# A decoder layer on one core: w_ada requests from ACT's queue to SP's, two norms two units later, and another order of window keys, exponentials and sums in the sample attention

## The chip, the cores and the metric

The kernel runs on one core of one Trainium2 chip. The core has five engines, each with a queue of its own: TensorE (PE, which multiplies matrices), VectorE (DVE), ScalarE (ACT), GpSimd (POOL) and SyncE (SP, used here only to request transfers). Transfers are carried by 16 DMA engines that all queues share. An engine that requests a transfer does so as an instruction in its own queue, and what is behind that instruction waits until it has gone out. The metric is the device time of one execution in microseconds, as the median over several runs.

## The reference

One step of a one-layer decoder. A prompt group (512 tokens) and a sample group (8 sequences of 8 new tokens, each with 2048 cached tokens in pages) go through the same weights: adaLN modulation and RMS norm, one wide input projection, two attention branches in parallel (forgetting attention, "FoX", and native sparse attention, "NSA", with a compressed, a selected and a sliding part), a gated mix, an output projection and a squared-ReLU MLP. Cut to what bears on this change:

```python
mod = einsum('bd,de->be', silu(c), w_ada) + b_ada          # shift, scale, gate of both norms
h   = rms_norm(x, norm1_g) * (1.0 + sc1) + sh1
z   = einsum('btd,dc->btc', h, w_in)

# each sample sequence: cached pages and the window's state
fox_all = concatenate([gather_pages(fox_pool, page_table), fox_rows])
nsa_all = concatenate([gather_pages(nsa_pool, page_table), nsa_rows])
kc, vc  = compressed_kv(nsa_all[:, :, 0], nsa_all[:, :, 1])      # compression of blocks of 32 tokens
o_fox   = softmax(fox_q . fox_k + cumulative log forget) . fox_v
o_nsa   = gate0 * o_compressed + gate1 * o_selected + gate2 * o_window   # window: last 512 tokens

mix = g_fox * (o_fox @ w_br_fox) + g_nsa * (o_nsa @ w_br_nsa)
x   = x + gt1 * (mix @ w_out)
y   = x + gt2 * (relu(norm2(x) @ w_up) ** 2 @ w_down)
```

At 8 sequences with 2048 cached tokens the selected part and the forgetting part read all keys of a sequence, 4 MB together.

## The kernel before

The program runs through stages, mostly one after the other on PE: a first stage that compresses the cached rows of the 8 sequences (to about 155 us), the input projection (to 285), the prompt attention (to 405), the sample attention (to 562), and then mix, output projection and MLP (to the end). Within each engine a scheduler puts instructions in order ahead of time; the code fixes an order between two instructions where it matters with `issue_after`, and the order written out in tables sets the rest. At run time every queue is strictly in order. A transfer on a hardware queue (SP and ACT) takes the next of eight semaphores in turn, and its request waits until the transfer that used the semaphore before has landed.

**First stage.** Its work is 48 units `u`, each twelve matmuls `hid` on half of the key or value rows of one or two sequences. ACT rounds the cached rows (`xh<-cpg`), DVE makes the remainder (`xl<-cpg,xh`). Other work is hung on the units by the table `todo` (from line 584 on): the adaLN matrix is multiplied in eight chunks of 1 MB (`ada_first`, in the order 4, 0, 5, 1, 6, 2, 7, 3, at units 27, 29, 32 and so on), each with a load of weights `wada` two chunks ahead (`ada_first_load`, two buffers), a copy `adap` on ACT and a turn `adat` on PE one unit later. In the same table stand the RMS norms of the five x tiles: `norm(k)` squares and sums a tile on ACT (`sq`), takes the root on DVE and scales on ACT (`x<-x,nrs`); `turned(k)` turns the tile on PE (`nt`) and copies it on ACT (`adw<-nt`). The rows of the last sequence's pages (`cpg`, eight loads of 128 KB) are requested by SP after the last x tiles.

**Sample attention.** `sample_attention` (line 1597) runs a loop over the sequences `b` = 0 to 7. The cached rows lie in three rooms (`fr` and `sr`, 2 MB each), so the loads of `b + 3` follow the last use of `b`. For each `b`: PE makes the scores `ss` (`sequence_scores`, line 1770, on 32 x 32 pieces), then scores with the new tokens `sn`; DVE takes the maximum and negates it; ACT takes the exponentials `sS`; PE turns the weights (`spn`, `sp`), ACT copies them (`spT`), and PE multiplies with the values (`so`). Meanwhile DVE turns the keys of the next sequence in place (`fr<-fr`, `sr<-sr`, one instruction for each quarter and each branch, and `oT<-D3b` for the log forget counts, copied to `CT` by ACT). All of these turns must be done before the next scores start.

The sliding window is done for two sequences at a time, at even `b`: PE turns the keys (`wk<-wr`, `window_keys`), ACT copies them (`wkt`), PE scores (`sw`, `window_scores`), DVE takes the maximum (line 1877), ACT takes the exponential (`scr<-scr,swst`, `window_weights`). `sequence_end` and `window_end` scale what `so` left for the sequence of two turns ago and for the window of the pair before (`OA`, `OAw`); the next values overwrite that bank, so `so` waits for them.

Of the kernel before, what the change touches and what calls it, by code (L numbers as in the profile page):

```python
# [10 lines left out]
AF = mybir.ActivationFunctionType  # L11
OP = mybir.AluOpType
# [33 lines left out]
class Step:  # L46
# [55 lines left out]
    def ts(self, out, a, s1, s2, op0, op1=None, **kw):  # L102
        if op1 is None:
            self.last_ts = self.nc.vector.tensor_scalar(out, a, s1, s2, op0=op0, **kw).ins
        else:
            self.nc.vector.tensor_scalar(out, a, s1, s2, op0=op0, op1=op1, **kw)

    def stt(self, out, a, s, b, op0, op1):
        return self.nc.vector.scalar_tensor_tensor(out, a, s, b, op0=op0, op1=op1)
# [135 lines left out]
    def late_constants(self):  # L245
        nc, I, ts, c, jp, field = self.nc, self.I, self.ts, self.const_tile, self.jp, self.field
        field("t_row", [(OP.bitwise_and, 7)])
        nc.vector.memset(c("ones", [P, P]), 1.0)
        field("prow", [])
        field("p_hi", [(OP.arith_shift_right, 3)])  # L250
        field("p31", [(OP.bitwise_and, 31)])
        field("g_row", [(OP.bitwise_and, 63), (OP.arith_shift_right, 5)])
        h_row = field("h_row", [(OP.bitwise_and, 63), (OP.arith_shift_right, 3)])

        sl = c("slope_i", [P, 1], I32)
        ts(sl, h_row, -1.0, 126.0, OP.mult, OP.add)
        ts(sl, sl, 23, None, OP.logical_shift_left)
        self.slope = sl.bitcast(F32)
        ts(c("identB", [P, P], BF16), jp, 0.0, None, OP.is_equal)
        ts(c("diagB", [P, P], BF16), jp, 0.0, NEG, OP.is_gt, OP.mult)  # L260
        ts(c("triU", [P, P]), jp, 0.0, None, OP.is_ge)
# [53 lines left out]

    def ada_first_load(self, pe, ch):
        w = self.adas[ch] = pe.tile([P, NK, 256], F32, tag="big", bufs=2, name=f"wada{ch}")
        if ch in (4, 0):
            self.ada_load(ch, w)
            return  # L320
        with self.tc.issue_after(self.last_high):
            self.ada_load(ch, w, "scalar")

    def ada_first(self, pe, ch):
        part = pe.tile([P, 256], F32, tag="adap", bufs=2, name=f"adap{ch}")
# [196 lines left out]
    def first_stage(self, pl, pe, hf):  # L522
# [12 lines left out]
        def norm(k):  # L535
            with self.tc.issue_after(self.last_high):
                self.norm_scaled(xs[k], 0, k, xs[k], pl.tile([P, D], BF16, tag="csx", name=f"sq{k}"))
            self.flipped = self.rooted

        def turned(k):  # L540
            t0, m = TILES[k]
            for h in range(2):
                self.act(hf[:, 4 * h:4 * h + 4, t0:t0 + m], self.norm_turned(xs[k], 0, k, h))
# [40 lines left out]
        todo = {u: [] for u in range(48)}  # L584
# [2 lines left out]
        todo[16] += [pinned(self.cmp_second_half)]  # L587
        todo[10] += [self.constants_turned, self.ada_turned, lambda: ends.update(b=self.cmp_bias(pe))]
        todo[12] += [lambda: self.cmp_bias_end(ends["b"])]
        for k, (n, u) in enumerate(((21, 24), (23, 26), (25, 28), (30, 32), (31, 33))):  # L590
            todo[n] += [lambda k=k: norm(k)]
            todo[u] += [lambda k=k: turned(k)]

# [18 lines left out]
        for k, u in enumerate((27, 29, 32, 34, 36, 38, 40, 42)):  # L612
            todo[u] += [lambda k=k: ends.update({k: self.ada_first(pe, ada[k])})]
            todo[u + 1] += [lambda k=k: ends[k]()]
            if k < 6:
                todo[u] += [wada(k + 2)]
            if k % 2:
                todo[max(u + 2, 34)] += [lambda k=k: self.modulate(0, hf, range(k - 1, k + 1)),
                                         lambda k=k: self.dma("gpsimd", self.hfd[:, k - 1:k + 1], hf[:, k - 1:k + 1])]
        self.lfg = {}  # L620
        for y, u in enumerate((34, 37)):
# [975 lines left out]
    def sample_attention(self, sp, ctx):  # L1597
# [37 lines left out]
        for b in range(NB):  # L1635
            n, odd = b // 2, b % 2
            if b and b + 2 < NB:
                self.key_prep(b + 2)
            self.sequence_scores(b, (lambda: self.values(b - 1, range(2, 4))) if b == last else None)
            if not odd and b:  # L1640
                for o in range(2):
                    self.window_keys(b + o)
            self.new_scores(b)
            if not odd:
                self.window_new(n)
            if not odd and b:
                self.values(b - 1, range(1, 4))
            if b == last:
                self.hL = self.keep.tile([P, 5 * D], F32R, tag="r2", bufs=1, name="hL2")[:, 0:NK * NT].rearrange("p (k t) -> p k t", k=NK)
                self.hH = self.rp.tile([P, NK, NT], F32R, tag="rp", name="hH")  # L1650
                self.tokens_load(range(4), self.CT[0:1, 0:4, None])
            self.sequence_max(b)
            if odd:
                self.window_turned(n)
            if b > 1:
                self.sequence_end(b - 2)
                if not odd:
                    self.window_end(n - 1)
            if b < last:
                with self.tc.issue_after(self.last_stat):  # L1660
                    self.key_turn(b + 1, (0, 1))
            if 0 < b < last and odd:
                self.values(b - 1, range(2, 4))
            if b == last - 1:
                self.mix_ahead()
            if odd:
                self.window_values(n)
                if b < last:
                    for o in range(2):
                        self.window_load(b + 1 + o, "gpsimd")  # L1670
                if b > 1:
                    self.pair_sums(n - 1)
            if b and b + 2 < NB:
                self.sample_load(b + 2, range(1 if b % 2 == 0 else 2, 4))
            if b < last:
                with self.tc.issue_after(self.last_stat):
                    self.key_counts(b + 1)
                    self.key_turn(b + 1, (2, 3))
            if b == last:
                self.sequence_end(b - 1)  # L1680
                self.window_end(n)
                ctx.close()
                self.mix_open()
                with self.tc.issue_after(self.last_exp):
                    self.w0 = self.gate_weights(0, 0)
            if b == 0:
                for o in range(2):
                    self.window_keys(o)
            if not odd and b:
                self.window_scores(n)  # L1690
            self.turn_weights(b)
            if b < last:
                with self.tc.issue_after(self.last_weights):
                    self.act(self.CT, self.ct)
            if b < last:
                self.values(b, range(1 if odd else 2))
            if b + 3 < NB:
                self.sample_load(b + 3, range(1 if odd else 2))
            if not odd:
                if b == 0:  # L1700
                    self.window_scores(n)
                self.window_weights(n)
            if b == 0:
                with self.tc.issue_after(self.last_stat):
                    self.sample_maps(maps)
# [146 lines left out]
    def sequence_end(self, b):  # L1852

        mx, dn, nm = self.stat.pop(b)
        d = self.small.tile([P, 1], F32, tag="sd", name=f"sd{b}")
        self.nc.vector.tensor_reduce(d, dn, axis=AX.X, op=OP.add)
        self.nc.vector.reciprocal(d, d)
        col = 128 * (b % 2)
        self.ts(self.OA[b % 2], self.sob[:, col:col + 64], d, self.GA[:, b:b + 1], OP.mult, OP.mult)

    def sums(self, b, sel, OA, first):

        for g in range(2):
            self.mm(self.acc[64 * g:64 * g + 64, 64 * b:64 * b + 64], OA, sel[g], first, not first)
# [14 lines left out]
    def window_weights(self, i):  # L1879
        st = self.wst[i]  # L1880
        self.tt(st[:, 2:3], st[:, 0:1], st[:, 1:2], OP.max)
        self.last_stat = self.nc.vector.tensor_scalar(st[:, 2:3], st[:, 2:3], -1.0, None, op0=OP.mult).ins
        self.act(self.SWt, self.SWt, AF.Exp, bias=st[:, 2:3], accum_out=st[:, 3:4])

    def window_turned(self, i):
        tb, tn = self.trb(f"spw{i}"), self.mmb(f"spwn{i}")
# [14 lines left out]
    def window_end(self, i):  # L1901
        st, col = self.wst.pop(i), 256 + 128 * (i % 2)
        self.nc.vector.reciprocal(st[:, 3:4], st[:, 3:4])
        w = self.OAw[i % 2]
        self.ts(w, self.sob[:, col:col + 64], st[:, 3:4], self.GB[:, 1, i:i + 1], OP.mult, OP.mult)
        self.stt(w, self.sob[:, col + 64:col + 128], self.GB[:, 0, i:i + 1], w, OP.mult, OP.add)

    def mix_open(self):

# [638 lines left out]
```

## Time and profile before

| | us |
| --- | --- |
| median of three runs | 1173.26 (1171.53 to 1177.72) |
| profiled execution | 1177.12 |
| its span | 1175.5 |
| first stage, 0 to 155: PE busy | 122.4 of 155 |
| input projection, 155 to 285: PE busy | 128.3 of 130 |
| prompt attention, 285 to 405: PE busy | 115.0 of 120 |
| sample attention, 405 to 562: PE busy | 142.3 of 157, mean granted clock 0.86 |
| rest, 562 to 1175.5: PE busy | 607.6 of 613.5 |

The profile is taken on one execution. A row of its timeline is: start, duration, engine, line, operation, output <- inputs, shape, how many instructions are merged into the row, and in brackets how long the engine had stood idle before it and what ended the idle time. "PEclk" and "granted clock" are the share of full speed at which TensorE was clocked. A busy PE at half clock is busy, but does half the work.

### The profile page before, as it was taken

Reading aid. Unit: us, or ns where it says so; the run is one execution under the profiler, and the core shown is the slowest. Engines: PE = TensorE matmul, PEld = TensorE weight load, DVE = VectorE, ACT = ScalarE, POOL = GpSimd, SP = SyncE. Lnnn points to the kernel's source line nnn. Section 1 sums busy time; section 2 is a strip of 40 time slices with the busy share of each in tenths; the row PEclk is TensorE's granted clock in tenths of the full one; section 3 lists DMA queues with packets and bytes.
Section 4 is the critical chain, followed back from the end, with each engine's and each line's share of the span. In section 5 each row is a group of like instructions: output and inputs, shape, how many; then the busy total and the mean of one; then the engine's idle time right before and its main releaser. Section 6 shows DMA issues by size and latency. Waiting matters only on the chain.

```text
span 1175.5 us, 24506 instructions
## 1 busy us (share of the span) xinstructions
PE 1115.5 (95%) x9161; PEld 950.5 (81%) x9161; DVE 779.3 (66%) x1904; ACT 524.9 (45%) x1107; POOL 241.5 (21%) x332
## 2 busy tenths in 40 slices
PE   3969999999999998998999999999999999999998
PEld 3966789998666654545999999998988889898896
DVE  6968666685788866744634346659856567575668
ACT  3547544454777754434523223464524234242330
POOL 6540000002211545420000000004123122231102
PEclk9998999999999998976999999999999999999999
DMA  9996485764976599964833344144214133231232
GB/s 223 294 273 199 146 249 191 239 213 133 296 223 211 147 310 364 352 244 108 208 81 82 83 125 126 46 142 128 84 42 126 37 106 106 64 118 48 79 112 85
DMA packets 165802, 189.40 MB, mean 161 GB/s; under 512 B 17546, under 2 KB 143955, under 8 KB 163507
## 3 DMA queue, kind: packets, MB, share of 16 engines
q1 hardware_dynamic: 144914, 142.87, 41.5%
q0 software_dynamic: 12352, 37.62, 9.5%
q10 hardware_dynamic: 8416, 7.34, 2.3%
q8 instruction: 72, 1.18, 0.4%
q14 instruction: 48, 0.39, 0.1%
HBM read 177.53 MB, written 31.16 MB: 178 GB/s over the span
## 4 chain that ended last, share of the span: by engine, by line
PE 81%; DVE 6%; DMA 6%; ACT 3%; issue 2%; SPq 1%; POOL 0%; POOLq 0%; DVEq 0%; ACTq 0%
PE dn L77 18%; PE z L77 9%; PE mg L77 8%; PE hid L77 6%; PE wo L77 4%; PE br L77 4%; PE up L77 4%; PE upx L77 3%; PE upv L77 3%; PE ss L77 3%; DMA cpg<-in_cache_nsa_kv 2%; DMA sr<-in_cache_nsa_kv 2%; PE so L77 2%; PE upy L77 2%; PE upz L77 2%
## 5 line engine op out<-in xcount | busy, mean ns | idle before, releaser
L100 DVE TENSOR_TENSOR acc<-acc,dn 128x512 f32<-128x512 f32 x66 | 44.6, 685 | 55.4 <-PE dn L77 55.3
L77 PE MATMUL mg<-hH,wml 128*128 128x288 f32 x256 | 75.2, 295 | 0.0
L77 PE MATMUL mg<-hH,wmh 128*128 128x288 f32 x256 | 75.1, 295 | 0.0
L77 PE MATMUL mg<-hL,wmh 128*128 128x288 f32 x256 | 72.8, 294 | 0.0
L77 PE MATMUL hid<-xh,w1hlk 128*128 128x256 f32 (+1 forms) x192 | 46.7, 336 | 19.6 <-ACT xh L112 19.6
L131 DVE TENSOR_TENSOR wml<-wmr,wmh 128x1024 fp32r<-128x1024 f32 x16 | 19.6, 1226 | 57.7 <-ACT wmh L112 57.7
L77 PE MATMUL z<-winh,h2r 128*128 128x264 f32 (+1 forms) x288 | 57.3, 288 | 0.0
L77 PE MATMUL z<-winh,h 128*128 128x264 f32 (+1 forms) x288 | 55.7, 283 | 0.0
L112 ACT ACTIVATE xh<-cpg 128x512 fp32r<-128x512 f32 x64 | 37.2, 623 | 37.2 <-PE hid L77 24.2
L131 DVE TENSOR_TENSOR xl<-cpg,xh 128x512 fp32r<-128x512 f32 x64 | 42.4, 684 | 14.8 <-ACT xh L112 14.6
L77 PEld LDWEIGHTS hid<-xh,w1hlk 128*128 128x128 f32 x192 | 32.8, 198 | 22.8 <-ACT xh L112 19.6
L112 ACT ACTIVATE u<-c 128x512 fp32r<-128x512 f32 x64 | 24.1, 433 | 59.4 <-PE dn L77 45.3
L2215 POOL TENSOR_TENSOR wur<-wur 128x512 f32<-128x512 f32 x12 | 18.9, 1573 | 149.7 <-DVE wu1l L131 55.4
L77 PEld LDWEIGHTS mg<-hH,wmh 128*128 128x128 f32 x256 | 48.2, 188 | 0.2
L77 PEld LDWEIGHTS mg<-hH,wml 128*128 128x128 f32 x256 | 48.1, 188 | 0.0
L77 PE MATMUL hid<-xh,w1hlv 128*128 128x256 f32 (+1 forms) x192 | 46.4, 334 | 1.2 <-ACT csx L112 1.2
L77 PEld LDWEIGHTS mg<-hL,wmh 128*128 128x128 f32 x256 | 47.3, 188 | 0.0
L77 PEld LDWEIGHTS z<-winh,h2r 128*128 128x128 f32 x288 | 45.5, 189 | 1.1 <-issue 0.4
L77 PEld LDWEIGHTS z<-winh,h 128*128 128x128 f32 x288 | 45.7, 189 | 0.0
L77 PE MATMUL z<-winl,h 128*128 128x264 f32 (+1 forms) x160 | 44.4, 284 | 0.5 <-DVE winl L131 0.5
L462 DVE STREAM_TRANSPOSE cpg<-cpg 128x1024 f32<-128x1024 f32 (+1 forms) x36 | 39.2, 1110 | 8.0 <-DMA cpg<-in_cache_nsa_kv 8.0
L77 PE MATMUL z<-winl,h2r 128*128 128x264 f32 (+1 forms) x160 | 44.5, 284 | 0.0
(839 smaller groups left out, 3561.3 us busy)
## 6 DMA issues: line engine op xcount, KB each, us to landing
adw<-in_w_ada SPq DMA_DIRECT2D x16, 1024.0 KB
foxD<-in_cache_fox_kv SPq DMA_DIRECT2D x128, 128.0 KB
wur<-in_w_up SPq DMA_DIRECT2D x32, 512.0 KB
wdr<-in_w_down SPq DMA_DIRECT2D x32, 512.0 KB
cpg<-in_cache_nsa_kv SPq DMA_DIRECT2D x64, 128.0 KB
cpg<-in_cache_nsa_kv POOLq DMA_DIRECT2D x64, 128.0 KB, 6.2
sr<-in_cache_nsa_kv SPq DMA_DIRECT2D x64, 128.0 KB
fr<-foxD SPq DMA_DIRECT2D x16, 512.0 KB
```

What stands on the lines that cost most here:

```text
L77: ins = self.nc.tensor.matmul(out, a, b, start=start, stop=stop, skip_group_check=True)
L100: self.nc.vector.tensor_tensor(out, a, b, op=op)
L112: return self.nc.scalar.activation(out, in_, f, **kw)
L131: self.splits.append((eng or self.nc.vector).tensor_tensor(l, x, h.bitcast(F32), op=OP.subtract).ins)
L462: self.flipped = self.nc.vector.transpose(v, v).ins
L2215: gp(a12, a12, a11, op=OP.subtract)
```

## The change

It has four parts.

1. `ada_first_load`: all loads of adaLN weights are requested by SP. Before, SP requested the first two (chunks 4 and 0) and ACT the other six.
2. The norms of the fourth and fifth x tile move from units 30 and 31 to units 32 and 33, and their turns from 32 and 33 to 34 and 35. What modulates them moves from unit 34 to 36 at the earliest.
3. Third sequence (`b` = 2): the turn of the window's keys goes from ahead of the new tokens' scores to behind the turn of the weights, and the window's scores from ahead of that turn to behind the values.
4. Later even sequences: the window's exponential goes behind the copies of the turned weights (`last_weights`), and the turns of the next sequence's log counts and second half of keys go behind the sums `OA` and `OAw` (`last_end`).

The core of the diff:

```diff
     def ada_first_load(self, pe, ch):
         w = self.adas[ch] = pe.tile([P, NK, 256], F32, tag="big", bufs=2, name=f"wada{ch}")
-        if ch in (4, 0):
-            self.ada_load(ch, w)
-            return
-        with self.tc.issue_after(self.last_high):
-            self.ada_load(ch, w, "scalar")
+        self.ada_load(ch, w)
...
-        for k, (n, u) in enumerate(((21, 24), (23, 26), (25, 28), (30, 32), (31, 33))):
+        for k, (n, u) in enumerate(((21, 24), (23, 26), (25, 28), (32, 34), (33, 35))):
             todo[n] += [lambda k=k: norm(k)]
             todo[u] += [lambda k=k: turned(k)]
...
-                todo[max(u + 2, 34)] += [lambda k=k: self.modulate(0, hf, range(k - 1, k + 1)),
+                todo[max(u + 2, 36)] += [lambda k=k: self.modulate(0, hf, range(k - 1, k + 1)),
...
             self.sequence_scores(b, (lambda: self.values(b - 1, range(2, 4))) if b == last else None)
-            if not odd and b:
+            ahead = not odd and b > 2
+            if ahead:
                 for o in range(2):
                     self.window_keys(b + o)
...
-                with self.tc.issue_after(self.last_stat):
+                with self.tc.issue_after(self.last_stat), self.tc.issue_after(self.last_end) if b > 1 else nullcontext():
                     self.key_counts(b + 1)
                     self.key_turn(b + 1, (2, 3))
...
-            if not odd and b:
+            if ahead:
                 self.window_scores(n)
             self.turn_weights(b)
+            if b == 2:
+                with self.tc.issue_after(self.last_weights):
+                    for o in range(2):
+                        self.window_keys(b + o)
             if b < last:
                 with self.tc.issue_after(self.last_weights):
-                    self.act(self.CT, self.ct)
+                    self.last_weights = self.act(self.CT, self.ct).ins
...
-                if b == 0:
+                if not ahead:
                     self.window_scores(n)
                 self.window_weights(n)
...
         self.ts(self.OA[b % 2], self.sob[:, col:col + 64], d, self.GA[:, b:b + 1], OP.mult, OP.mult)
+        self.last_end = self.last_ts
...
-        self.act(self.SWt, self.SWt, AF.Exp, bias=st[:, 2:3], accum_out=st[:, 3:4])
+        with self.tc.issue_after(self.last_weights):
+            self.act(self.SWt, self.SWt, AF.Exp, bias=st[:, 2:3], accum_out=st[:, 3:4])
...
-        self.stt(w, self.sob[:, col + 64:col + 128], self.GB[:, 0, i:i + 1], w, OP.mult, OP.add)
+        self.last_end = self.stt(w, self.sob[:, col + 64:col + 128], self.GB[:, 0, i:i + 1], w, OP.mult, OP.add).ins
```

How the instructions stand on the engines, at three places. First ACT's queue in the first stage, from the copy of the chunk 4 (`adap_1455`) on, as one piece of the difference (`-` before alone, `+` after alone):

```order
 L112 ACTIVATE adap_1455<-ada_1456 128x256
-L155 DMA wada_1466<-in_w_ada 128x8x256
 L112 ACTIVATE adw<-nt_20_1483 128x4x128
 L112 ACTIVATE adw<-nt_21_1489 128x4x128
 L112 ACTIVATE xh_213<-cpg_979 128x512
-L112 ACTIVATE sq_1630,nss_3_1631<-x_1372 128x1024
 L112 ACTIVATE xh_205<-cpg_979 128x512
 L112 ACTIVATE xh_209<-cpg_979 128x512
 L112 ACTIVATE adap_1601<-ada_1602 128x256
-L155 DMA wada_1612<-in_w_ada 128x8x256
```

The requests of chunks 5 (`wada_1466`) and 1 (`wada_1612`) leave ACT, and so does the square of the fourth x tile from among the three splits; it comes back behind the copy of chunk 5. On SP the requests stand as follows, behind the last sequence's pages (`cpg_1516`); the first of the six, `wada_1466`, stands ahead of these pages, right behind the fifth x tile:

```order
 L155 DMA cpg_1516<-in_cache_nsa_kv 128x1x256
-L155 DMA lfD<-lfg_1831 128x512
+L155 DMA wada_1612<-in_w_ada 128x8x256
+L155 DMA wada_1714<-in_w_ada 128x8x256
+L155 DMA wada_1806<-in_w_ada 128x8x256
+L155 DMA wada_1928<-in_w_ada 128x8x256
+L155 DMA lfD<-lfg_1810 128x512
+L155 DMA wada_1985<-in_w_ada 128x8x256
 L155 DMA lfD<-lfg_1956 128x512
```

Four requests now stand ahead of the first store of the log forget rows (`lfD`), and one between it and the second.

Last DVE at `b` = 4, where the sums of sequence 2 (`OA_6404`) and of the window of sequences 2 and 3 (`OAw_6407`) stand against the turns for sequence 5 (`fr_6498`, `sr_6499`). Before:

```order
L1758 STREAM_TRANSPOSE oT<-D3b 128x512
L1765 STREAM_TRANSPOSE fr_6498<-fr_6498 128x4x128
L1765 STREAM_TRANSPOSE sr_6499<-sr_6499 128x4x128
L1765 STREAM_TRANSPOSE fr_6498<-fr_6498 128x4x128
L1765 STREAM_TRANSPOSE sr_6499<-sr_6499 128x4x128
L106 TENSOR_SCALAR OA_6404<-so,sd_7616,GA 128x64
L106 TENSOR_SCALAR OAw_6407<-so,swst_7042,GB 128x64
L1856 TENSOR_REDUCE sd_8115<-ss_4_7497 128x1
```

And with the change:

```order
L106 TENSOR_SCALAR OA_6404<-so,sd_7616,GA 128x64
L106 TENSOR_SCALAR OAw_6407<-so,swst_7030,GB 128x64
L1857 TENSOR_REDUCE sd_8115<-ss_4_7497 128x1
L109 SCALAR_TENSOR_TENSOR OAw_6407<-so,GB,OAw_6407 128x64
L1759 STREAM_TRANSPOSE oT<-D3b 128x512
L1766 STREAM_TRANSPOSE fr_6498<-fr_6498 128x4x128
L1766 STREAM_TRANSPOSE sr_6499<-sr_6499 128x4x128
L1766 STREAM_TRANSPOSE fr_6498<-fr_6498 128x4x128
L1766 STREAM_TRANSPOSE sr_6499<-sr_6499 128x4x128
```

The five turns have moved behind the two sums and the reduction `sd`. The same holds at `b` = 2 and 6.

More of the change, by code (lines that the diff above doesn't have):

```diff
@@ L105, in ts @@
         else:
-            self.nc.vector.tensor_scalar(out, a, s1, s2, op0=op0, op1=op1, **kw)
+            self.last_ts = self.nc.vector.tensor_scalar(out, a, s1, s2, op0=op0, op1=op1, **kw).ins
     def stt(self, out, a, s, b, op0, op1):
```

## The prediction

> **What bounds the kernel now.** First the page: where the engines are busy, at what clock TensorE runs, and who stands on the chain that ended last.
>
> ```profile
> PE 1115.5 (95%) x9161; PEld 950.5 (81%) x9161; DVE 779.3 (66%) x1904; ACT 524.9 (45%) x1107; POOL 241.5 (21%) x332
> PEclk9998999999999998976999999999999999999999
> PE 81%; DVE 6%; DMA 6%; ACT 3%; issue 2%; SPq 1%; POOL 0%; POOLq 0%; DVEq 0%; ACTq 0%
> ```
>
> TensorE bounds the kernel: 95% busy, 81% of the chain. Nothing here takes away a matmul, so the time can only come from PE's idle stretches and from stretches at a lower clock. The clock row dips twice, in slice 4 (near 90 us) and in slices 19 and 20 (about 500 to 560 us). These are the first stage and the sample attention, the two places that the change touches. The windows view, taken around the dips, has per row: stretch, its length, the busy time of PE, PEld, DVE, ACT and POOL (instructions), granted clock, DMA share, GB/s.
>
> ```profile
> 84.50:94.70 10.20, 4.07 (x17) 3.88 (x18) 4.92 (x18) 6.03 (x12) 0.00 (x0) 0.50 1.10 251
> 460.00:463.40 3.40, 0.69 (x6) 0.42 (x4) 1.31 (x4) 0.60 (x1) 1.29 (x4) 1.00 1.04 403
> 470.30:500.90 30.60, 26.70 (x554) 16.16 (x552) 22.20 (x66) 14.29 (x32) 14.82 (x29) 1.00 1.00 347
> 497.50:500.90 3.40, 0.87 (x8) 0.63 (x6) 3.40 (x10) 0.25 (x1) 2.64 (x5) 1.00 0.93 324
> 500.96:518.02 17.06, 16.29 (x261) 7.91 (x261) 7.59 (x25) 6.19 (x14) 4.25 (x9) 0.50 0.65 231
> 535.09:555.57 20.48, 19.21 (x285) 10.68 (x286) 6.20 (x27) 6.06 (x15) 1.17 (x3) 0.50 0.26 78
> ```
>
> The half clock after 500.96 follows a window in which PE did little (0.87 of 3.4 us), and so does the short one near 464, which the change's first sample part concerns (0.69 of 3.4). Then PE runs at half clock for 17 us, and once more for 20, although it is busy again. An idle gap is thus paid twice.
>
> **First stage.** These rows are of ACT, PE and SP's queue in time, and one of the chain.
>
> ```profile
> 59.30 1.64 SPq L155 DMA_DIRECT2D wada<-in_w_ada  x2
> 77.87 1.07 PE L77 MATMUL ada<-wada,adw 128*32 128x256 f32 x16 [0.41 <-DMA wada<-in_w_ada]
> 78.44 9.66 DMA x<-in_x_prompt
> 79.98 0.53 SPq L155 DMA_DIRECT2D x<-in_x_sample  x1
> 83.18 0.41 ACTq L155 DMA_DIRECT2D wada<-in_w_ada  x1
> 83.64 1.08 ACT L112 ACTIVATE adw<-nt 128x512 f32<-128x512 f32 x2 [9.38 <-DMA cpg<-in_cache_nsa_kv]
> 88.12 1.06 ACT L112 ACTIVATE sq<-x 128x1024 bf16<-128x1024 f32 x1 [2.89 <-DMA x<-in_x_prompt]
> 90.63 0.69 PE L83 MATMUL adat<-identF,adap 128*128 128x128 f32 x2 [10.05 <-ACT adap L112]
> 95.99 1.14 ACT L112 ACTIVATE x<-x,nrs 128x1024 f32<-128x1024 f32 x1
> 97.03 1.14 ACT L112 ACTIVATE xh<-cpg 128x512 fp32r<-128x512 f32 x2
> 97.19 1.10 PE L83 MATMUL nt<-identF,x 128*128 128x128 f32 x8
> 98.21 1.07 PE L77 MATMUL ada<-wada,adw 128*32 128x256 f32 x16
> ```
>
> ACT stands from 74.26 (83.64 less the 9.38 us idle) at the request of wada5, which goes out at 83.18: it is held until a page load of SP lands (the releaser in brackets). Then it waits 2.89 us for the fourth x tile (its norm's square, `sq`). PE waits 10.05 us for what ACT does behind both, until 90.63. The change takes both waits out of ACT: the request goes to SP, the norm two units later. ACT is then free at 74.3, PE goes on at 80.6 without its 10 us gap, does the two units that it did from 90.63 to 97.19, and at about 87 needs wada5.
>
> So the next wait is wada5's landing. SP asks for it behind the last x tile, at 80.6 or little later. The fourth x tile, in front of it in the queue, takes 9.66 us and lands at 88.10; one MB more at the 251 GB/s of this stretch takes 4.2 us: **92.3**. Bounds: 88.1, with the x tile; 98.0, after the 17.4 us that wada0 took (second request of the pair at about 60.4, used at 77.87). The matmul `ada` moves from 98.21 to 92.3: 5.9 us gained. Against it stands a new wait. The norm's scale on ACT (1.14 us) now comes behind two `xh` splits (1.14 us for two) that wait for PE's unit 34, and PE's turn of this tile comes right behind that unit: 2.3 us, and the 1.1 us of the turn itself now lies behind the gap, not in it. 5.9 - 3.4 = **2.5 us** (from -3.2 to 6.7). The eight page loads behind wada5 on SP land some 4 us later; I put this at nothing, because PE has earlier pages to work on until then (uncovered, it would be those 4 us, within the range); ACT's other five requests, 0.4 us each, were beside PE's work.
>
> A rule of the Trainium skill speaks against this part: "DMA: Bandwidth & Descriptors", section "Issuing engines are not separate DMA queues", says that requests of all engines end on the same 16 DMA engines, and that choosing the engine saves only the time of issuing. By that rule alone the move would be worth 0.4 us a request. This trace shows the other price: 8.9 us in which the issuing engine stood at the request.
>
> **Sample attention.** The next rows are PE's around the third sequence (b=2), POOL's requests, how long the window rows `wr` take to land, and one piece of the chain.
>
> ```profile
> 457.69 2.33 POOL L155 DMA_DIRECT2D sr<-in_cache_nsa_kv  x4 [1.27 <-DMA fr<-foxD]
> 458.30 8.56 DMA sr<-in_cache_nsa_kv
> 461.51 0.66 PE L83 MATMUL wk<-identF,wr 128*128 128x128 f32 x4 [1.47 <-DMA wr<-in_state_win_kv]
> 464.25 1.11 PE L83 MATMUL wk<-identF,wr 128*128 128x128 f32 x4 [2.08 <-DMA wr<-in_state_win_kv]
> 465.29 0.37 PE L77 MATMUL sn<-knT,bdF 128*64 128x64 f32 x1
> 482.91 1.09 POOL L155 DMA_DIRECT2D wr<-in_state_win_kv  x2 [4.07 <-PE so L77]
> DMA to landing us min/median/max: 6.1/7.1/8.8
> ```
>
> PE has ended the scores at 460.0 and stands at `wk` for window rows; `sn`, from which softmax starts, comes at 465.29. With `wk` behind the weight turns, `sn` starts 5.3 us earlier and the rows land under other work. What is late next is the fourth sequence's keys: the last of four requests goes out at 459.5, lands 8.56 us later at 468.1, and one turn (0.6 us) on, its scores start at 468.7. Before they start at 474.62 (chain, below): **5.9 us**. The next pair's `wr` is asked for behind `so` of b=3, so it moves along.
>
> ```profile
> 474.62 5.17 PE ss L77 x67
> 480.76 2.35 PE so L77 x120
> 496.46 1.91 PE L83 MATMUL sp<-identF,sS 128*128 128x128 f32 x16
> 496.67 0.67 DVE L1758 STREAM_TRANSPOSE oT<-D3b 128x512 f32<-128x512 f32 x1
> 496.90 0.19 ACT L112 ACTIVATION_READ_ACCUMULATOR sS<-sS,ss 128x1 f32 x1
> 499.64 0.30 DVE L106 TENSOR_SCALAR OA<-so,sd,GA 128x64 f32<-128x64 f32 x1
> 501.20 0.32 PE L77 MATMUL so<-fr,spT 128*32 128x64 f32 x2 [2.83 <-DVE swst L100]
> 501.22 0.15 DVE L1882 TENSOR_SCALAR swst<-swst 128x1 f32<-128x1 f32 x1
> 503.89 8.63 PE ss L77 x68
> 514.19 3.98 PE so L77 x120
> 535.84 0.15 DVE L1882 TENSOR_SCALAR swst<-swst 128x1 f32<-128x1 f32 x1
> 538.12 4.32 PE ss L77 x33
> ```
>
> At b=4 `so` waits 2.83 us for the sums (`OA`, `OAw`), which stand behind five turns from 496.67 to 499.64. Ahead of these they are done 3 us earlier, when PE's own transposes `sp` (496.46 to 498.37) have just ended. One wait is added: the reduction of `sd`, behind which all five turns now stand, needs ACT's last exponential. That ended at 497.09, and DVE comes there at 496.67 + 0.5 = 497.2: nothing, at most 0.3 us. The sliding exponential no longer holds back ACT's copies `spT`. The next scores then start when DVE ends this work, at 501.37 (the turns are the same in number), not at 503.89: **2.5**. At b=6 the same sum is 538.12 less 535.99: **2.1**.
>
> The gap between PE's matmuls proper, `sp` taken out, falls from 4.7 us (496.46 to 501.20) to about 2, so I expect full clock behind it. At b=5 the scores then take 5.17 for 8.63 and `so` 2.35 for 3.98: 3.46 + 1.63 = **5.1**. At b=7 the scores alone give **3.5**; what follows them is ACT's and DVE's chain, unchanged. Sum: 5.9 + 2.5 + 5.1 + 2.1 + 3.5 = 19.1, with the first stage 21.6. From the profiled execution's 1177.1 (span 1175.5 and 1.6 around it) this makes 1155.5. That execution lay 3.86 us above the median of 1173.26, so the median comes to **1151.7**. What follows the sample attention is PE-bound and moves along whole.
>
> The page "TensorE: Matmul & The Clock Gate" of the Trainium skill, Part 1, section "What's actually happening", lets the clock fall after one idle window of about 3.4 us and rise after one busy one; Part 4 adds that transposes do not count like other work. The falls agree (0.87 us, all of it `sp`, in the window from 497.5). The rise does not: five busy windows passed in 500.96 to 518.02. By the page's fall a gap of 2 us is safe, as in the forecast; by its rise the slower rival below could not be, for one busy window would end it; by this trace it can, and it keeps a small chance.
>
> **Rivals.**
> - *The window rows become the next wait.* DMA share is 1.00 from 470 to 501 us, 347 GB/s. If the earlier work finds no free transfer time, the rows of b=4 land when they did (the second of the two requests at 483.5 + 7.1 = 490.6), while PE comes for them 5.9 us earlier. With 1 us of slack before, `sn` there gains 1 us, not 5.9, and the gap of 5 us brings half clock back at b=5: 21.6 - 4.9 - 5.1 = 11.6, so 1161.7. For it: the full share. Against: the request moves along, and landing takes 8.8 us at most.
> - *The clock falls once more elsewhere*, most likely at b=2, where `sp` and `wk` (1.9 + 1.1 us of transposes) now stand in a row: 5.1 lost, 1156.8.
> - *wada5 lands late* and the first stage loses: 98.0 gives 2.5 + 3.2 less, 1157.4. That the request merely waits on another queue, so the part does nothing, is this case's near end (1154).
> - *Slower.* The clock falls at b=2 and does not come back: in 500.96 to 518.02 scores at 32 x 32 never raised it, only a window full of `so`. With the waits between them gone no such window may form. Then steps b=3, 4 and 6 each pay 5.1 us, and the 5.1 and 3.5 of b=5 and 7 are not won: 21.6 - 8.6 - 15.3 = -2.3, and `sp` and `wk` at half clock in each even step 1 us more: 1177 to 1179; with a late wada5 1183. It decides from the third such step on.
>
> **How the numbers follow.** Forecast 0.55 (alone 1146 to 1156: wada5 at 88.1 takes off 4.2, loads 4 late add 4); window rows 0.14; clock once 0.11; wada5 late 0.08; slower 0.05; 0.07 for loads and clock together, near 1167. The range, 1144 to 1167, leaves out the slower case and the ends. A measurement of this kernel tells 0.5% (5.9 us) from no change: faster 0.87, same 0.09 (the case near 1167 and part of the slower one), slower 0.04.
>
> **What would show it.** ACT busy from 74 to 84 us and PE's gap there under 8 us; `ada` near 92; scores of b=3 near 466 (468.7 less 2.5); no half clock between 450 and 550; `so` of b=4 right behind `sp`. Wrong would be: a wait of PE for `wr` at b=4, half clock at b=5, or SP standing at a request that wada5's neighbours wait behind.

## The result, and the profile after

| | before | after |
| --- | --- | --- |
| median of 18 runs each, us | 1177.30 (1167.89 to 1182.52) | 1167.38 (1160.67 to 1176.50) |
| ratio after to before | | 0.9921, 95% interval 0.9894 to 0.9947 |
| profiled execution, us | 1177.12 | 1169.14 |
| its span and mean granted clock | 1175.5, 0.976 | 1167.5, 0.986 |

The change is 0.8% faster, clear of noise: 9.9 us between the medians where 21.6 were forecast. (The median before is now over more runs and stands 4 us higher than the one the forecast started from; the ratio compares kernels of the same chip and hour. One later run of the changed kernel, 1214.6 us at a mean clock of 0.86, was a slow one and is left out of its ratio below.)

The clock row of the page after stands against the one of before in the prediction.

```profile
PE 1111.7 (95%) x9161; PEld 947.0 (81%) x9161; DVE 780.0 (67%) x1904; ACT 524.8 (45%) x1107; POOL 242.4 (21%) x332
PEclk9998999999999998899999999999999999999999
```

The dip of the first stage is still there. The dip of the sample attention is shallower (8899 where 8976 stood), but it has not gone. Where PE starts each piece, from its timeline rows:

| PE starts | before | after | difference |
| --- | --- | --- | --- |
| `ada` of chunk 5 | 98.21 | 92.29 | -5.9 |
| `ada` of chunk 6 | 115.16 | 114.88 | -0.3 |
| scores of b=0 | 426.34 | 428.51 | +2.2 |
| b=1 | 441.98 | 444.25 | +2.3 |
| b=2 | 454.56 | 460.77 | +6.2 |
| b=3 | 474.55 | 474.81 | +0.3 |
| b=4 | 486.53 | 493.94 | +7.4 |
| b=5 | 503.82 | 507.46 | +3.6 |
| b=6 | 521.27 | 521.54 | +0.3 |
| b=7 | 538.05 | 534.95 | -3.1 |
| first `mg` of the mix | 558.86 | 551.14 | -7.7 |

From b=4 to the mix all of the forecast came: 72.3 us became 57.2. Before b=4 the change has lost 7.4 us. First the first stage, by the chain of what ended last (start, length, what).

```profile
78.69 13.56 DMA wada<-in_w_ada
92.29 1.94 PE ada L77 x16
94.22 4.11 PE hid L77 x12
...
101.42 1.15 ACT xh L112 x2
102.57 1.05 ACT x L112
103.62 0.04 issue
103.67 1.09 PE nt L83 x8
...
109.47 1.15 ACT xh L112 x2
110.62 0.28 ACT adw L112
```

The load of chunk 5 lands at 92.25; the forecast said 92.3. The `xh` splits and the scale `x` then hold up `nt`, as forecast. Two things were not in the sum: after the gap, `ada` takes 1.94 and the unit 4.11 us at half clock, and the tile's second round on ACT holds PE once more at 109.5. In sum 22.6 us go from chunk 5 to chunk 6, where it was 17.0.

Between chunk 6 and the scores of b=0 another 2.5 us are lost: a wait of 1.6 us for `adw` in the input projection (at 241 us) and a half clock of 3.4 us in the prompt attention (from 301 us). The profile before has neither, but profiles of kernels without the first-stage parts have one or both, so no run shows that they belong to the change.

Then the sample attention, by windows (the columns are those of the prediction).

```profile
444.70:448.10 3.40, 2.83 (x34) 0.62 (x26) 3.37 (x22) 0.87 (x2) 2.58 (x5) 1.00 0.95 348
448.10:458.30 10.20, 10.20 (x166) 5.42 (x165) 6.97 (x20) 3.35 (x8) 5.04 (x10) 0.50 1.04 378
475.40:478.80 3.40, 1.79 (x24) 0.62 (x23) 0.69 (x5) 0.87 (x2) 1.07 (x2) 1.00 1.04 368
478.80:489.00 10.20, 10.20 (x111) 3.88 (x101) 4.02 (x14) 1.32 (x5) 1.82 (x4) 0.50 0.56 203
489.10:550.00 60.90, 55.26 (x1259) 33.49 (x1255) 40.08 (x119) 32.37 (x72) 19.19 (x37) 1.00 0.77 252
```

The half clock behind b=4 and b=6 is gone: from 489 to 550 the clock is full. In its place stand two stretches of 10.2 us at new places, at b=1 and at b=3. Neither place had one in the profile before, and no line of the change touches b=1. Before, the scores of b=1 ran mostly in these two windows, at full clock.

```profile
443.00:446.40 3.40, 3.26 (x54) 1.01 (x58) 3.33 (x23) 0.87 (x2) 2.15 (x4) 1.00 1.01 375
446.40:449.80 3.40, 3.40 (x103) 1.97 (x91) 2.83 (x13) 0.82 (x3) 1.60 (x3) 1.00 1.03 378
```

In the changed kernel the windows ahead of the two stretches were not idle either: PE was busy for 2.83 and for 1.79 of 3.4 us. The chain shows what stands in the second one, and the steps behind it.

```profile
471.86 0.87 PE wk L83 x8
472.73 1.03 PE so L77 x64
473.76 1.12 PE sw L77 x4
474.88 0.98 PE ss L77 x4
475.86 1.61 issue
477.47 8.72 PE ss L77 x62
...
493.96 5.38 PE ss L77 x68
...
507.46 5.30 PE ss L77 x68
...
516.92 1.09 PE sp L83 x10
518.01 2.14 issue
520.15 0.88 PE sp L83 x6
```

`wk` comes behind the weights without a wait, as planned. But the scores of b=3 stop after four matmuls for something that the profile does not name ("issue"), and go on at half clock: 8.72 us where 5.17 were. A second such stop costs 2.1 us in the middle of `sp` at b=5.

### The profile page after: what moved, and what is told of

It is laid out like the page before. It is cut to its first block, busy times and chain, and to the rows that moved or that the text cites. A ratio compares the mean times of both kernels' runs of the same rounds, so it can differ in the third digit from the quotient of the medians.

```text
span 1167.5 us, 24517 instructions
## 1 busy us (share of the span) xinstructions
PE 1111.7 (95%) x9161; PEld 947.0 (81%) x9161; DVE 780.0 (67%) x1904; ACT 524.8 (45%) x1107; POOL 242.4 (21%) x332
## 4 chain that ended last, share of the span: by engine, by line
PE 85%; DVE 5%; DMA 4%; ACT 4%; issue 2%; SPq 1%; DVEq 0%; POOL 0%; ACTq 0%
PE dn L77 18%; PE mg L77 9%; PE z L77 9%; PE hid L77 7%; PE wo L77 4%; PE br L77 4%; PE ss L77 4%; PE up L77 4%; PE upx L77 3%; PE upv L77 3%; PE ada L77 2%; PE upy L77 2%; PE upz L77 2%; PE upu L77 2%; PE so L77 1%
```

## The experiments

Two theories were set against each other. **Clock**: the parts do what was worked out, and the missing time is half clock at new places that differ from execution to execution. **Own waits**: the change has waits of its own, the same in every execution. Each kernel ran 6 or 12 times, beside the kernel before on one chip. "Clock" is the median of the runs' mean granted clocks; the runs of the kernel before had 0.976 to 0.980.

| kernel | ratio to before | 95% interval | median us | clock |
| --- | --- | --- | --- | --- |
| changed kernel again | 0.9894 | 0.9831 to 0.9956 | 1164.1 | 0.989 |
| first-stage parts alone | 1.0086 | 1.0051 to 1.0121 | 1186.3 | 0.971 |
| sample parts alone | 0.9887 | 0.9832 to 0.9941 | 1164.6 | 0.990 |
| keys part alone | 0.9998 | 0.9966 to 1.0029 | 1175.9 | 0.978 |
| order part alone | 0.9881 | 0.9838 to 0.9925 | 1164.7 | 0.988 |
| sample parts and requests by SP | 0.9897 | 0.9854 to 0.9940 | 1165.3 | 0.986 |
| sample parts and norms later | 0.9945 | 0.9911 to 0.9979 | 1169.5 | 0.984 |
| changed kernel and 36 fillers | 0.9929 | 0.9893 to 0.9964 | 1168.5 | 0.991 |
| before and fillers in two gaps | 0.9946 | 0.9919 to 0.9974 | 1171.9 | 0.985 |
| sample parts and 12 fillers | 0.9861 | 0.9823 to 0.9900 | 1163.6 | 0.990 |
| order part and 6 fillers | 0.9848 | 0.9811 to 0.9885 | 1162.3 | 0.992 |

### The changed kernel again

No edit.

> The changed kernel itself once more, for a second profile and more runs. Theory clock: every part does what was worked out, and the missing 12 us are half-clock stretches at new places (b=1, b=3, prompt attention in the first profile), which differ from execution to execution; then this profile shows them at other places or not at all, and over the runs the time follows the mean granted clock by about 0.46 us for each us at half clock. Theory own waits: the change brings waits of its own (first stage, SP's order, loads), the same in each execution; then the same places are slow again and the runs spread without regard to the clock.

Its median is 3 us lower, and its interval overlaps the first one. In its profile the place at b=1 is not slow, and the one at b=3 is. These are the windows at those two places.

```profile
442.10:445.50 3.40, 2.97 (x80) 1.16 (x71) 3.29 (x10) 1.82 (x4) 2.42 (x5) 1.00 0.97 308
472.80:476.20 3.40, 2.69 (x30) 0.95 (x29) 0.16 (x1) 0.59 (x2) 1.73 (x4) 1.00 1.04 377
476.20:486.40 10.20, 10.20 (x165) 5.25 (x165) 6.62 (x19) 3.35 (x8) 2.95 (x7) 0.50 0.95 338
```

At b=1 a window with 2.97 us busy (80 instructions, `so` among them) kept the clock. At b=3 one with 2.69 (30 instructions, scores) lost it. Over the runs the time follows the clock: in the first 18 of the changed kernel the correlation of time with mean clock is -0.89, in the 23 of before that ran beside this one -0.91, where six at 0.984 and more took 1170 to 1172 us and those at 0.975 and less 1178 to 1186. From the slope of -1086 us per unit of mean clock, 1 us at half clock, which is 1/2334 of a unit, costs 0.47 us; the slope of those 23 runs of before, -890, makes it 0.38. So theory clock holds for the spread; the stop in the scores of b=3, after four matmuls, is there in both profiles (1.6 and 1.3 us), which is theory own waits at that one place.

### The first-stage parts alone, and the sample parts alone

The first kernel has the lines of `ada_first_load` and of the table `todo` of the diff, the second all others.

> The kernel before with the first-stage parts alone (requests on SP, norms two units later). Theory clock: 0.3 us faster as in the profile after (the gain of 5.9 us at the third chunk is given back by unit 36), ratio 0.997 to 1.003. Prediction: 2.5 us faster, 0.998. Theory own waits: the part costs some 2 us later on, ratio 1.002.

> The kernel before with the sample parts alone (third sequence's window keys, exponentials last, sums ahead of turns). Theory clock: the whole gain, ratio 0.989 to 0.994, the best runs near 1158. Theory own waits: more than the whole change, 0.988 to 0.990, since the first stage's cost is gone.

The first-stage parts alone are 0.9% **slower**, more than either theory said. In their profile the span is 8.3 us longer than before. The input projection starts at 157.5 against 154.1, 3.4 us late, and the sample attention adds 3.8 us, with 51 us at half clock against 44. The page's row shows both: the first stage has a second stretch at half clock, and the dip of the sample attention is wider. No line of these parts stands in the sample attention; why the clock was lower there, and in the median of the runs (0.971), is open.

```profile
PEclk9997999999999998777999999999999999999999
```

The sample parts alone are as fast as the whole change, 0.9887, and the intervals of the two overlap: as far as these tell, the whole gain is theirs.

### The four parts apart

Two kernels split the sample parts. One has the third sequence's window keys behind the weights (`if b == 2` and `ahead = not odd and b > 2`) and nothing else. The other has the exponential behind `last_weights` and the key turns behind `last_end`:

```diff
-            ahead = not odd and b > 2
+            ahead = not odd and b
...
-            if b == 2:
-                with self.tc.issue_after(self.last_weights):
-                    for o in range(2):
-                        self.window_keys(b + o)
```

> The kernel before with the third sequence's window keys behind the weights alone. Theory terms (each part gives its own term, 5.9 us here): b=3's scores start 5 to 6 us earlier than in the kernel before, counted from b=0's, and the ratio is 0.994 to 0.997. Theory clock (the gain of all parts is the half clock that they avoid, and the waits themselves count little): the half-clock time falls by a third or less of what the whole change takes off (57 to 31 us), ratio 0.997 to 1.001.

> The kernel before with the sliding exponentials last and the sums ahead of the key turns alone. Theory terms: 2.5 + 2.1 us of waits and 5.1 + 3.5 of half clock behind them, ratio 0.987 to 0.991, half clock behind b=4 and b=6 gone. Theory clock: nearly the whole of what the sample parts gave (0.989), with half-clock time near 30 us; a half clock may still stand behind b=1 and b=2.

The keys part alone gives nothing (0.9998). The chain of its profile shows where the 5.3 us went that its new-token scores start earlier.

```profile
458.14 8.92 DMA sr<-in_cache_nsa_kv
467.06 0.03 issue
467.08 0.05 DVEq L1770
467.13 0.04 issue
467.18 0.71 DVE sr L1770
467.89 0.23 DVE OA L106
...
468.84 1.94 PE so L77 x64
470.77 1.57 PE sw L77 x4
472.34 0.97 PE ss L77 x9
```

DVE reaches the last turn of b=3's keys earlier and waits for their load, which lands at 467.1 (the forecast: 468.1). The sums stand behind that turn, so `so`, `sw` and the scores come behind the load too, at 472.3, with `so` at half clock (1.94 for 1.10). So the gain needs the sums ahead of the turn. The order part alone, 0.9881, gives as much as all sample parts. In its profile the clock falls at b=2 and in the scores of b=4, but not behind the sums of b=4 and b=6. So nothing is left to the keys part in the whole change either, as far as the intervals tell.

Two more split the first-stage parts, each on top of the sample parts.

> The sample parts and all requests of w_ada by SP, norms at their old units. Before ran the sample parts alone (1164.6 us). Theory own waits of the first stage: ACT is free of the request but still stands at the fourth x tile until 88, so PE waits as before and the third chunk comes at 97 to 99; 0 to 1 us slower by the end of the first stage. Prediction's sum: nothing without the norms' move. Ratio 0.988 to 0.992.

> The sample parts and the norms two units later, requests of w_ada still by ACT. ACT then stands at the request until 83.2 but not at the x tile: PE's gap ends near 85, the third chunk still waits for its load, issued at 83.2, to 95 or 96; then the new wait of 3.4 to 5.6 us. Theory own waits: 1 to 3 us slower by the end of the first stage than the sample parts alone, ratio 0.990 to 0.993; if it is the requests on SP that cost, none: 0.988.

These rows of PE are the chunks 5, 1 and 6 with the turn of the fourth x tile, first with the requests by SP, then with the norms later.

```profile
98.36 1.09 PE L83 MATMUL nt<-identF,x 128*128 128x128 f32 x8
99.39 1.07 PE L77 MATMUL ada<-wada,adw 128*32 128x256 f32 x16
...
116.34 1.07 PE L77 MATMUL ada<-wada,adw 128*32 128x256 f32 x16
```

```profile
97.60 1.07 PE L77 MATMUL ada<-wada,adw 128*32 128x256 f32 x16
107.02 1.09 PE L83 MATMUL nt<-identF,x 128*128 128x128 f32 x8 [2.04 <-ACT x L112]
...
118.23 1.07 PE L77 MATMUL ada<-wada,adw 128*32 128x256 f32 x16
```

With the requests alone, chunk 5 comes at 99.4 (97.2 in the sample parts alone) and chunk 6 17.0 us later, as always: nothing gained, since ACT waits for the x tile instead. With the norms alone, chunk 5 comes at 97.6 and chunk 6 20.6 us later: the norms' move itself costs 3.7 us in this profile and gains nothing. Its ratio of 0.9945 is the worst of the kernels that have the sample parts, though its interval still touches those of the others.

### Fillers: keeping the clock without removing a wait

A filler is a matmul of 128 x 128 by 512 into a bank that is overwritten afterwards; nothing reads it.

```diff
+    def fill(self, pb, n):
+        w = self.W2.rearrange("p b n -> p (b n)")
+        for _ in range(n):
+            self.mm(pb, w[:, 0:P], w[:, 0:512], True, True)
```

In the changed kernel:

```diff
+        if b % 2:
+            self.fill(pbs[0], 4)
         for h in (0, 2):
...
+            if i == 0 and (b == 1 or b % 2 == 0):
+                self.fill(tb, 4)
```

> The changed kernel with 36 matmuls more that compute nothing used, four each ahead of the turned weights of b=1 and of the even sequences and ahead of the scores of the odd ones, at some 0.25 us each, where PE waits. Theory clock: fewer half-clock stretches, mean clock 0.990 and more, ratio 0.980 to 0.988. Theory own waits: the matmuls cost what they take where PE does not wait, 3 to 9 us: ratio 0.994 to 1.000.

The clock rose to 0.991, but the ratio is 0.9929. In its profile the sample attention ran at full clock but for one window, and took 117.7 us from b=0's scores to the mix, the same as the changed kernel's second profile with 10.2 us at half clock. The fillers cost what they saved. The ratio fell between the ranges of the two theories, and its interval reaches into that of own waits. The direct test puts them where PE is sure to wait, in the kernel **before**:

```diff
+            if b in (4, 6):
+                self.fill(self.mmb(f"fl{b}"), 10)
             if b < last:
                 self.values(b, range(1 if odd else 2))
```

> The kernel before, with ten matmuls more that compute nothing used (some 2.4 us) in the 3 us in which PE waits for the sums at b=4 and b=6; the waits themselves stay. Theory clock: the half clock behind b=4 and b=6 goes, 5.1 + 3.5 us and some 35 us of half-clock time, ratio 0.990 to 0.994. Theory waits (the gain of the order part is the wait for the sums and what stands behind it on ACT and DVE): no gain, ratio 0.999 to 1.002.

Here no wait is taken away and no order changed, and the kernel is 0.54% faster. The chain behind the two gaps, and the window over b=5:

```profile
505.81 5.02 PE ss L77 x65
...
511.79 2.35 PE so L77 x120
...
517.73 5.30 PE ss L77 x68
```

```profile
502.00:519.00 17.00, 15.30 (x355) 9.06 (x357) 10.83 (x35) 9.03 (x20) 8.81 (x17) 1.00 0.94 320
```

The scores of b=5 take 5.02 and `so` 2.35 us, where the kernel before had 8.63 and 3.98. From b=4's scores to the mix it takes 60.2 us, against 72.3 before and 57.2 with the change. So in these profiles 12.1 of the change's 15.1 us from b=4 on can be had by the clock alone; the shorter waits account for the other 3, by subtraction. This execution (1167.9 us, clock 0.991) was the second fastest of its twelve; by the medians the fillers gave 7.2 us, so the share of the clock alone is smaller over the runs than in this profile.

The last two try the fillers at b=1 and b=3, with the sample parts (three ahead of the scores of both and of the turned weights of b=1 and 2) and with the order part (three ahead of the scores of both).

> The sample parts alone with twelve such matmuls: three ahead of the turned weights of b=1 and b=2, three ahead of the scores of b=1 and b=3, which cost 0.7 us each where PE does not wait. Theory clock: the falls at b=1 and b=3 are rarer, median half clock under 20 us, ratio 0.983 to 0.988, no worse than the sample parts alone (0.989). Theory own waits: 1 to 3 us slower than the sample parts alone, 0.990 to 0.992.

> The order part alone (exponentials last, sums ahead) with six such matmuls, three ahead of the scores of b=1 and of b=3. Theory clock: the fall at b=1 goes, ratio 0.983 to 0.988. Theory own waits: 1 us slower than the order part alone (0.988).

With the sample parts the twelve fillers gave 0.9861, in the range of theory clock, but the interval overlaps that of the sample parts alone. The order part with six fillers is the fastest measured, 0.9848. Its interval overlaps those of the order part alone and of the changed kernel run again; only against the first measurement of the change (0.9894 at the lowest) is it clear. That the fillers add anything to the order part is likely by the clock (0.992 against 0.988) but not settled.

## Why the prediction was wrong

The forecast was 1151.7 us and 21.6 gained; 9.9 came by the medians, and the time missed the range's end of 1167.0 by 0.4. In the first profile the mix starts 7.7 us earlier, so 13.9 of the 21.6 are missing: 4.7 up to the scores of b=0 and 11.1 from there to b=4, while from b=4 on it came 1.9 better than forecast. By its steps:

- **What bounds it** was right: PE, its gaps and its clock. That "an idle gap is paid twice" is what the gap fillers showed.
- **First stage, 2.5 us**: the step that failed is the sum "5.9 - 3.4". The 5.9 came (92.29), with some luck: the request went out at 78.7, not 80.6, and in the three other profiles with both parts chunk 5 came at 93.3 to 94.4. What stands against it was 5.6, not 3.4: the half clock behind the 7.5 us of waiting for the load, 2.0 us on two pieces, was not priced, although the row of the kernel before showed half clock at that place; nor was the second wait for ACT, 1.5 us. The turn and smaller pieces came 1.3 cheaper. Alone, the parts put the input projection 3.4 us later, and the kernel 0.9% slower.
- **Keys of b=3, 5.9 us**: in the first profile the step from b=2's scores to b=3's is shorter by just that (+6.2 became +0.3), but the tenth is luck. I had b=3's scores wait for the landing of its keys and start near 466; they started at 474.8, and the chain between the two scores is PE's own work and softmax, with no load in it. What I had not seen is that the gain needs the sums ahead of the turns: alone the part gave 0. And b=3 behind it then lost 7.1 us to the stop (1.6) and the half clock, so that it gave nothing in the whole.
- **Sums ahead, exponential last, full clock at b=5 and b=7: 2.5 + 5.1 + 2.1 + 3.5 = 13.2**: 15.1 in the profile from b=4 on. The mechanism was right, and the order part alone gives all that the change gave.
- **"So I expect full clock behind it"** is the step that failed most. It was right for the two gaps that it was made for. All other gaps I put at nothing, because the one profile before showed no fall there, and that is where most of the 11.1 us went: 3.9 at b=1, and 7.1 at b=3 with the stop. Why the clock fell at b=1, behind a window that was busy for 2.83 of 3.4 us, stays open. Half clock came at b=1 in four of the ten profiles without fillers at that place, and between b=2 and b=4 in nearly all. By the runs' mean clocks, the half-clock time (twice the time by what the clock lacks to 1) fell from 47 to 57 us to 26 to 32; I had counted on none left from 450 to 550 us.
- **The rival "the clock falls once more elsewhere"** at 1156.8 is what happened, more than once; 0.11 was far too low for it. The case put near 1167 has the measured number by luck only: its late loads did not come. The rivals of the window rows and of no return did not come: PE did not wait for `wr` at b=4, and the clock rose after 10.2 us both times. Of the signs of being wrong one did show: SP stood at the eight page loads until 92.8, and the next request of `w_ada` went out at 92.9 (90.3 before); its chunk came at 104.7 without a wait for it.
- **The start**: I took 3.86 us off because one profiled execution lay above the median of three. Over 18 runs that execution is the median, so these 3.86 us were a mistake of their own. Without it the time would have lain inside the range, but the gain of 21.6 would have been as wrong. (The two low digits of the clock row are the 18th and 19th, not the 19th and 20th; the times given for them are right.)

## What to carry to other kernels

Where a kernel runs in and out of half clock, one profile is one draw: look at the mean granted clock of all runs, and price every gap that could lose the clock, not only those that lost it in the profile at hand. Split a change of several parts on the chip: here, as far as the intervals tell, one part gave everything, two nothing, and one cost time. Before moving work out of an engine's way, look at what it will stand behind at its new place; the norms moved two units later took with them a chain through ACT that PE had not felt before.

## What the runs showed of the hardware that I had not expected

- **A busy window can lose the clock.** At b=1 the clock fell after 2.83 of 3.4 us busy, with scores on 32 x 32 pieces and a stop of 0.6 us between them. Seven of thirteen profiles have a stop of 0.2 us or more at that place. The clock fell in four of them, with stops of 0.36 to 0.57 us and a window that held scores and the stop alone. It held in the second run of the changed kernel, whose window reached back to `so` and `sw`, and in the two kernels with fillers in the gaps (the changed kernel's and the one before's), whose windows held 0.2 us of it. The page "TensorE: Matmul & The Clock Gate" of the Trainium skill, Part 1, section "What's actually happening", names an idle window as the cause of a fall; these windows were not idle. That the scores count for little is my reading of it; no run tried it by itself.
- **The clock changes on a grid.** In each of the 13 profiles the moments at which the granted clock changes lie whole steps of 3.413 us apart (in the changed kernel the falls at 89.69, 301.32, 448.09 and 478.81 us: 62, 43 and 9 steps). Stretches at half clock last whole steps, from 3.4 to 20.5 us. Where the grid stands against the kernel's start differs from profile to profile, from 0.07 to 3.30 us. So the same gap can lie within one step in one execution and be parted between two in the next. That this is why the executions of one kernel differ is likely, but no run tried it.
- **PE can stop with no releaser, beside a transfer of instructions.** The stop at 475.9 us has no releaser. In the 3 us around it the DMA view of the changed kernel shows the instruction queues at work:

```profile
q8 instruction: 1, 0.02, 2.1%
q14 instruction: 1, 0.01, 0.8%
```

  The 16 KB of queue 8 begin at 474.99 and end at 476.02, and PE goes on 1.5 us later; at b=5 they run from 517.61 to 518.77 and PE stands from 518.01 to 520.15. Such stops of about 1 us and more came in the sample attention of all kernels that have the order part, one to four in a profile and 1.1 to 3.5 us each; of the others, only the keys part alone had one (1.0 us). Of these 20 stops 19 began 0.2 to 1.5 us after a transfer of 16 KB on queue 8 had begun. But the 13 profiles hold 243 such transfers in the sample attention, and most passed without a stop. That the stop is a wait for instructions was not tried by itself.
